# First mixer of a hybrid backbone step: decay tables by blocks on ScalarE, softmax scaling on ScalarE, SiLU held until the decay exponentials, attention's copies behind retention

## The chip, the cores and the metric

The program runs on one core of a Trainium2 chip. The metric is the device time of one launch in microseconds (us). The engines have short names in the profile: PE is TensorE (matmul; PEld is its weight load), DVE is VectorE, ACT is ScalarE, POOL is GpSimd, SP is SyncE, which here issues nearly all of the DMAs. Below, `hp` is a pair of heads (0 to 3), so hp1 is the second pair.

## The reference, cut to what matters

One inference step over two layers, for 256 latent and 128 context tokens of width 1024, all in fp32. Every layer is a mixer and a SwiGLU channel mixer (called FFN below); a conditioned shift, scale and gate and a norm stand before and behind each. The change is in the mixer of layer 0, which runs two groups of eight heads side by side on one input projection:

```python
z = h @ w_in                       # qa, ka, va | qb, kb, vb, gb
# attention: local window with a position bias, plus the context, in one softmax
s = jnp.concatenate([s_loc, s_ctx], axis=-1)
p = jax.nn.softmax(s, axis=-1)
o = p_loc @ v_loc + p_ctx @ v_ctx
# retention, forward and backward, per head with decay log_g < 0
diff = pos[:, None] - pos[None, :]
dmask = where(diff >= 0, exp(log_g * diff), 0)
o = (q @ k.T * dmask) @ v + (q * q_dec) @ state
ob = _rmsnorm(o_f + flip(o_b)) * silu(gb)
out = concatenate([oa, ob]) @ w_out
```

## The kernel before

All 384 tokens stay in SBUF, features on the partitions. A product with a weight matrix keeps fp32 accuracy by splitting: the weight chunk `wr` (8 tiles of 128x128) becomes `wh`, a rounded copy that ACT makes (line 244), plus `wl`, the rest, which DVE makes by a subtraction (line 252); the activation is `hh` plus `hl` in the same way. Each tile then costs three matmuls, hh by wh, hh by wl and hl by wh (line 226). 216 weight chunks of 512 KB pass through three buffers.

A second kind of weight, `mraw` (1 MB chunks in two buffers), gives the conditioning. Most of its chunks are worked off by DVE with a multiply and sum (`mscr<-mraw,msb`, line 265), as filler work of low priority; the pair of chunks 16 and 17 and the pair 18 and 19 go to PE instead (`bank<-mraw,sc`, four or eight rows at a time, function `mod_pe`), and the small product `ca,mev` finishes a pair.

The mixer of layer 0 runs these products in turn: queries and keys of attention (E1), its values (E2), values of retention (E5), the last of attention's queries (E3), queries and keys of retention (E4), the gate (E6), and then the output product (OUT). Beside them run small generators, one instruction at a time: `attention(hp)`, `probabilities(h)` (bias, maximum, exponentials, then the scaling of the 128x896 table `as` by the reciprocal sums `sm`, three line 258 instructions), `attended(hp)`, `retention(hp)`, `retention_norm`, `gate_out` (SiLU of the gate `va`, 128x1536) and `attention_out` (the copies hh and hl of attention's output `qa`).

`retention(hp)` first gets the keys and queries with their halves swapped by eight small DMAs (`ro<-qk`), rotates on DVE (`ro<-ro,cse`, `qk<-qk,cse`, `qk<-qk,ro`), multiplies the queries by their decay (`qd<-qd,qk`; PE uses it in `qd,s`), and then builds for each of its two heads a 128x384 table of decays, `dt` in the code and `scr` in the profile: a line 258 instruction multiplies the forward distances E_DP by the head's rate, a line 265 instruction adds the backward distances E_DM times the other rate, ACT takes the exponential of the whole, and an identity is added in the middle 128 columns. In the left 128 columns all forward distances are 0, in the right 128 all backward ones. The table masks the products of queries and keys (`qk 64x256` on PE, then `ro<-bank,scr` and `at<-bank,scr` on DVE), and `ro,vb` and `at,vb` multiply by the values.

`retention_norm` follows when all four pairs are there: a sum of squares on PE (`scr,cse 32x96`), a square root on ACT, a reciprocal and a spreading on DVE, and for each pair a broadcast on PE (`scr,cse 128x384`), two multiplications on DVE (the second by the SiLU of the gate) and the copies hh and hl. OUT's second half needs these. Behind OUT stands the Step: the norm after the mixer, the addition to `x`, and the norm before the FFN, with `acc,ca`, `rs,cb` and others as its small products. Some `cb,ca` products there have no use for the result; they only keep PE busy.

What comes first on each engine is set in the Python program, before the kernel runs: each generator is a stream with a priority, and a planner (`Machine.run`, a list scheduler) again and again emits the instruction that could start first by its own table of costs, at ties the one with the smaller priority number. On the chip each engine runs its list in that order, and waits on semaphores for what its instruction needs. So a change of the cost, kind or priority of a few instructions in one stream can reorder the lists from there on, and the planner's clock carries it into later stages. Attention has priority 3.0, retention 3.5, `retention_norm`, `gate_out` and `attention_out` 2.5, weight splitting 1 or 6, and the filler on DVE 8. A DMA is on SP's one list.

Of the kernel before, what the change touches and what calls it, by code (L numbers as in the profile page):

```python
# [32 lines left out]
AF = mybir.ActivationFunctionType  # L33
# [3 lines left out]
P = 128  # L37
# [4 lines left out]
NT = NS + NP  # L42
# [435 lines left out]
def emit_all(nc, tc, ctx, io, outs):  # L478
    cp = ctx.enter_context(tc.tile_pool(name="cp", bufs=1))
    pp = ctx.enter_context(tc.tile_pool(name="pp", bufs=1, space=bass.MemoryType.PSUM))  # L480
    M, I = Machine(), Build(nc)
    MUL, ADD, SUB = ALU.mult, ALU.add, ALU.subtract
# [622 lines left out]
            ev.add(("gb", m - 24))  # L1105
        banks.give(b)

    L0.attended = L0.exps = 0

    def attention(hp):  # L1110

# [11 lines left out]
    def probabilities(h, res, b0, b1):  # L1123
        s, mx, sm = res
        yield lambda: len(L0.biases) > 0 and L0.biases[0][0] == h
        bias = L0.biases.popleft()[1]
        yield I.tt(s[:, 0:NT], b0[:, :NT], bias[:, 0], ADD)
        yield I.reduce_max(mx[:, 2:3], b0[:, NT:512])
        yield I.tt(s[:, NT:768], b1[:, :NT], bias[:, 1], ADD)
        banks.give(b1)  # L1130
        L0.bias.give(bias)
        yield I.reduce_max(mx[:, 0:2], s[:, :768].rearrange("p (t c) -> p t c", t=2))
        yield I.ts(mx, mx, -1.0, MUL)
        yield I.act(s[:, 768:896], b0[:, NT:512], AF.Exp, bias=mx[:, 2:3], accum=sm[:, 2:3])
        banks.give(b0)
        for tb in range(2):
            t = s[:, NT * tb:NT * tb + NT]
            yield I.act(t, t, AF.Exp, bias=mx[:, tb:tb + 1], accum=sm[:, tb:tb + 1])
        L0.exps += 1
        yield I.recip(sm, sm)  # L1140
        for c0, c1, n in ((0, NT, 0), (NT, 768, 1), (768, 896, 2)):
            yield I.ts(s[:, c0:c1], s[:, c0:c1], sm[:, n:n + 1], MUL)
        pt, = yield from L0.pt.take()
        b0, b1 = yield from banks.take(2)
        for kb in range(2):
            for tb in range(2):
                c = NT * tb + P * kb
                yield I.transpose(b0[:, 256 * kb + P * tb:256 * kb + P * tb + P], s[:, c:c + P], ident)
        yield I.act(pt[:, :512], b0)
        banks.give(b0)  # L1150
        for n, c in enumerate((256, NT + 256, 768)):
            yield I.transpose(b1[:, P * n:P * n + P], s[:, c:c + P], ident)
        yield I.act(pt[:, 512:], b1[:, :NT])
        banks.give(b1)
        L0.heads.give(res)
        L0.ptof[h] = pt
        if 2 * (h // 2) in L0.ptof and 2 * (h // 2) + 1 in L0.ptof:
            M.spawn(attended(h // 2), 3, margin=M_ATT)

    L0.ptof = {}  # L1160

    def attended(hp):

# [16 lines left out]
    def retention(hp):  # L1180

        res, = yield from L0.ret.take()
        s0, kd, ro, qd, at = res
        st = at[:, 0, :P]
        yield lambda: "ret" in ev
        yield I.dma(s0, io["s0r"][:, hp])
        ap_, ats = kd.rearrange("p a b c -> p (a b c)").rearrange("p (a b) -> p a b", a=2), (ro, at)
        yield lambda: "ret" in ev and ("qb", hp) in ev and ("kb", hp) in ev and len(L0.vb_in) == 3
        qk, vb, cse = L0.qk, L0.vb, L0.cse
        q, k = qk[:, hp, 0], qk[:, hp, 1]  # L1190

        for a in range(0, P, 16):
            yield I.dma(ro[a:a + 16], qk[a ^ 16:(a ^ 16) + 16, hp, :, :NS])

        b, = yield from banks.take()
        yield I.transpose(b[:, :P], k[:, NS:NT], ident)
        yield I.tt(kd, b[:, :P].rearrange("p (j c) -> p j c", j=2).unsqueeze(2).to_broadcast([P, 2, 2, 64]),
                   L0.kdec[:, 2 * hp:2 * hp + 2].unsqueeze(3).to_broadcast([P, 2, 2, 64]), MUL)
        yield tuple(I.mm(b[:, P + 64 * j:P + 64 * j + 64], kd[:, j].rearrange("p a b -> p (a b)"),
                         vb[:, 2, 64 * (2 * hp + j):64 * (2 * hp + j) + 64]) for j in range(2))  # L1200
        yield I.act(st, b[:, P:NS])
        banks.give(b)
        yield I.dma(outs["sret"][:, P * hp:P * hp + P], st)

        lat = qk[:, hp, :, :NS]
        wide = lambda o: cse[:, o:o + NS].unsqueeze(1).to_broadcast([P, 2, NS])
        yield I.tt(ro, ro, wide(E_SIN), MUL)
        yield I.tt(lat, lat, wide(E_COS), MUL)
        yield I.tt(lat, lat, ro, ADD)

        for d, e0 in ((0, E_TF), (1, E_TB)):
            yield I.act(qd[:, d], cse[:, e0:e0 + NS], AF.Exp, scale=L0.rdp[:, hp, d:d + 1])
        yield I.tt(qd, qd, q[:, :NS].unsqueeze(1).to_broadcast([P, 2, NS]), MUL)
        po, = yield from banks.take()
        for d in range(2):
            yield I.mm(po[:, :NS], s0[:, d], qd[:, d], d == 0, False)

        rows = [slice(64 * j, 64 * j + 64) for j in range(2)]
        dts = yield from scr.take(2)
        for j, dt in enumerate(dts):  # L1220

            h = 2 * hp + j
            yield I.ts(dt, cse[:, E_DP:E_DP + NT], L0.rdb[:, 0, h:h + 1], MUL)
            yield I.stt(dt, cse[:, E_DM:E_DM + NT], L0.rdb[:, 1, h:h + 1], dt, MUL, ADD)
            yield I.act(dt, dt, AF.Exp)
            yield I.tt(dt[:, P:2 * P], dt[:, P:2 * P], ident, ADD)
        bs = yield from banks.take(2)
        yield tuple(I.mm(bs[j][:, NS * n:NS * n + NS], k[rows[j], P * s_:P * s_ + P], q[rows[j], :NS])
                    for n, s_ in ((0, 1), (1, 0)) for j in range(2))
        for j in range(2):  # L1230
            for n in range(2):
                yield I.tt(ats[j][:, n], bs[j][:, NS * n:NS * n + NS], dts[j][:, P * n:P * n + NS], MUL)
        yield tuple(I.mm(bs[j][:, :P], k[rows[j], NS:NT], q[rows[j], NS:NT]) for j in range(2))
        for j in range(2):
            yield I.tt(ap_[:, j], bs[j][:, :P], dts[j][:, P:2 * P], MUL)
        banks.give(*bs)
        scr.give(*dts)
        head = lambda b, j: vb[:, b, 64 * (2 * hp + j):64 * (2 * hp + j) + 64]
        for n, s_ in ((0, 1), (1, 0)):
            yield tuple(I.mm(po[64 * j:64 * j + 64, :NS], head(s_, j), ats[j][:, n], False, n == 1) for j in range(2))  # L1240
        yield tuple(I.mm(po[64 * j:64 * j + 64, NS:NT], head(2, j), ap_[:, j]) for j in range(2))
        L0.exps += 1
        yield I.act(q, po[:, :NT])
        banks.give(po)
        L0.ret.give(res)
        ev.add(("ob", hp))
# [27 lines left out]
        scr.give(t)  # L1274

    def gate_out():
        yield lambda: all(("gb", i) in ev for i in range(4))
        yield I.act(L0.sg, L0.sg, AF.Silu)
        ev.add("silu")

# [340 lines left out]
    with tc.tile_pool(name="l0", bufs=1) as lp:  # L1621
# [13 lines left out]
        for hp in range(4):  # L1635
            M.spawn(retention(hp), P_RET + 0.01 * hp, margin=M_RET)
        M.spawn(retention_norm(), 2.5, margin=M_RN)
        M.spawn(attention_out(), 2.5)
        M.spawn(gate_out(), 2.5)

        def stores():
# [75 lines left out]
```

## Time and profile before

| | us |
|---|---|
| median of 3 runs | 1129.93 |
| lowest and highest run | 1129.28, 1131.42 |
| the profiled execution's own time | 1129.32 |
| its span in the trace | 1127.5 |

The profile is of one execution. Times in its rows count from the start of its span. "Busy" is the time in which at least one instruction of an engine ran; "idle before" is the time an engine stood still ahead of an instruction, and "<-" says which engine or transfer ended that wait. PEclk is TensorE's granted clock as a share of its full 2.4 GHz. The last row of a wait list counts "us in total, times, longest us". The first mixer's attention and retention lie at about 57 to 198 us, its norm and the output product at 198 to 241, the Step at 241 to 252, the first FFN follows to 590, the second layer's mixer lies at 590 to 800, and the last FFN ends the span.

### The profile page before, as it was taken

How to read it: one execution, taken by the hardware profiler on the slowest of the kernel's cores; microseconds unless marked ns; L12 is line 12 of the kernel's file. 1: busy time of each engine (PE TensorE's matmuls, PEld its weight loads, DVE VectorE, ACT ScalarE, POOL GpSimd, SP SyncE). 2: the span in 40 equal slices, each digit the busy share in tenths (PEclk: the TensorE clock that was granted, in tenths of full speed). 3: DMA queues.
4: the chain of work that ended last, by engine and by line, in shares of the span. 5: the costliest groups of instructions: out<-in, count | busy, mean ns of one | idle time of the engine just before them, and what ended most of it. 6: DMA issues, size and time to landing. Idle time of an engine off the chain costs nothing.

```text
span 1127.5 us, 18541 instructions
## 1 busy us (share of the span) xinstructions
PE 1088.1 (97%) x7180; PEld 1011.7 (90%) x7180; DVE 819.9 (73%) x1524; ACT 541.8 (48%) x1002; POOL 136.7 (12%) x143
## 2 busy tenths in 40 slices
PE   6999999899999999999999999999999999999996
PEld 5778888679999999999887988888989999999995
DVE  2598888687989999995888489996786444444334
ACT  3585555368333333323765456655666333333321
POOL 1220000000000000234024046352000000000001
PEclk9999999999999999999999999999999999999998
DMA  9966544534667677565341322223224333333431
GB/s 351 359 215 215 168 149 132 215 136 152 233 241 240 238 245 240 205 227 167 135 156 62 127 85 85 76 76 103 94 84 141 122 123 129 123 123 129 131 112 56
DMA packets 49688, 180.44 MB, mean 160 GB/s; under 512 B 6560, under 2 KB 13728, under 8 KB 43072
## 3 DMA queue, kind: packets, MB, share of 16 engines
q1 hardware_dynamic: 49536, 179.18, 46.7%
q8 instruction: 56, 0.92, 0.3%
q14 instruction: 32, 0.26, 0.1%
q0 software_dynamic: 64, 0.08, 0.0%
HBM read 174.79 MB, written 3.41 MB: 158 GB/s over the span
## 4 chain that ended last, share of the span: by engine, by line
PE 77%; DVE 15%; issue 3%; DMA 2%; ACT 1%; SPq 1%; POOL 0%; DVEq 0%; ACTq 0%; POOLq 0%
PE bank L226 76%; DVE wl L252 3%; DVE mscr L265 2%; DMA mraw<-in_w_mod 2%; DVE XB L252 1%; DVE XA L252 1%; SPq L291 1%; DVE TA L252 1%; DVE scr L258 1%; PE bank L230 1%; DVE scr L252 1%; DMA ro<-qk 0%; DVE ZW L252 0%; DVE ac L282 0%; POOL ZW L250 0%
## 5 line engine op out<-in xcount | busy, mean ns | idle before, releaser
L226 PE MATMUL bank<-hh,wh 128*128 128x384 f32 (+1 forms) x1248 | 431.0, 345 | 0.0
L226 PE MATMUL bank<-hh,wl 128*128 128x384 f32 (+1 forms) x1248 | 425.4, 341 | 0.0
L226 PE MATMUL bank<-hl,wh 128*128 128x384 f32 (+1 forms) x1248 | 391.0, 344 | 0.0
L252 DVE TENSOR_TENSOR wl<-wr,wh 128x1024 fp32r<-128x1024 f32 x216 | 272.5, 1262 | 128.2 <-ACT wh L244 128.0
L244 ACT ACTIVATE wh<-wr 128x1024 fp32r<-128x1024 f32 x216 | 228.1, 1057 | 151.2 <-PE bank L226 106.0
L226 PEld LDWEIGHTS bank<-hh,wh 128*128 128x128 f32 x1248 | 237.9, 191 | 6.4 <-ACT scr L244 2.4
L226 PEld LDWEIGHTS bank<-hh,wl 128*128 128x128 f32 x1248 | 237.5, 190 | 0.9 <-issue 0.3
L226 PEld LDWEIGHTS bank<-hl,wh 128*128 128x128 f32 x1248 | 232.4, 189 | 5.6 <-issue 2.0
L265 DVE SCALAR_TENSOR_TENSOR mscr<-mraw,msb 128x1024 bf16<-128x1024 f32 x128 | 159.4, 1245 | 3.5 <-ACT msb L244 2.4
L226 PE MATMUL bank<-gh,wl 128*128 128x384 f32 x352 | 118.2, 336 | 1.8 <-DVE wl L252 1.8
L226 PE MATMUL bank<-gh,wh 128*128 128x384 f32 x352 | 117.6, 334 | 0.0
L226 PE MATMUL bank<-gl,wh 128*128 128x384 f32 x352 | 117.6, 334 | 0.0
L226 PEld LDWEIGHTS bank<-gh,wl 128*128 128x128 f32 x352 | 66.1, 188 | 3.4 <-DVE wl L252 3.4
L226 PEld LDWEIGHTS bank<-gl,wh 128*128 128x128 f32 x352 | 66.1, 188 | 0.0
L226 PEld LDWEIGHTS bank<-gh,wh 128*128 128x128 f32 x352 | 66.1, 188 | 0.0
L244 ACT ACTIVATE fs<-bank 128x384 f32<-128x384 f32 x44 | 21.1, 492 | 90.2 <-PE bank L226 90.2
L252 DVE TENSOR_TENSOR fs<-bank,fs 128x384 f32<-128x384 f32 x44 | 24.1, 556 | 39.4 <-PE bank L226 39.4
L244 ACT ACTIVATE gh<-fs 128x384 fp32r<-128x384 f32 x44 | 22.5, 519 | 57.7 <-DVE fs L252 57.6
L244 ACT ACTIVATE scr<-bank 128x384 f32<-128x384 f32 x44 | 21.9, 499 | 58.2 <-PE bank L226 58.2
L250 POOL TENSOR_TENSOR rB<-x,fy 128x384 f32<-128x384 f32 x1 | 1.9, 1877 | 387.3 <-DVE fy L258 387.3
L250 POOL TENSOR_TENSOR x<-x,fy 128x384 f32<-128x384 f32 x4 | 4.5, 1152 | 346.4 <-DVE fy L252 346.4
L250 POOL TENSOR_TENSOR ZW<-XB,TA 128x192 f32<-128x192 f32 x48 | 37.9, 810 | 31.8 <-ACT XA L244 17.4
(249 smaller groups left out, 1330.1 us busy)
## 6 DMA issues: line engine op xcount, KB each, us to landing
mraw<-in_w_mod SPq DMA_DIRECT2D x48, 1024.0 KB, 5.7
wr<-in_w_ffn_in SPq DMA_DIRECT2D x88, 512.0 KB, 3.3
wr<-in_w_ffn_out SPq DMA_DIRECT2D x44, 512.0 KB, 3.3
wr<-in_w_in_odd SPq DMA_DIRECT2D x40, 512.0 KB, 3.3
wr<-in_w_in_even SPq DMA_DIRECT2D x28, 512.0 KB, 4.4
wr<-in_w_out_even SPq DMA_DIRECT2D x8, 512.0 KB, 4.0
wr<-in_w_out_odd SPq DMA_DIRECT2D x8, 512.0 KB, 3.3
bias<-in_bias SPq DMA_DIRECT2D x8, 384.0 KB, 3.8
```

The costliest lines, as they stand in the source:

```text
L226: return Op("PE", lambda: self.nc.tensor.matmul(out, lhsT=lhsT, rhs=rhs, start=start, stop=stop), [out], [lhsT, rhs], cost + 0.004)
L230: return Op("PE", lambda: self.nc.tensor.transpose(out, in_, ident), [out], [in_], 0.11)
L244: return Op("ACT", lambda: self.nc.scalar.activation(out, in_, func, **kw), outs, ins, 0.1 + width(in_) / 1200, table)
L250: return Op("POOL", lambda: self.nc.gpsimd.tensor_tensor(out=out, in0=a, in1=b, op=op), [out], [a, b], 0.12 + n * 0.0021)
L252: return Op("DVE", lambda: self.nc.vector.tensor_tensor(out=out, in0=a, in1=b, op=op), [out], [a, b], 0.06 + n / 960)
L258: return Op("DVE", lambda: self.nc.vector.tensor_scalar(out=out, in0=a, scalar1=s1, scalar2=s2, op0=op0, **kw), [out], ins, 0.19 + width(o ...
L265: return Op("DVE", lambda: self.nc.vector.scalar_tensor_tensor(out=out, in0=a, scalar=s, in1=b, op0=op0, op1=op1, **kw), outs, ins, 0.1 + ...
L291: return Op("SP", lambda: self.nc.sync.dma_start(out, in_), [a for a in here if a is out], [a for a in here if a is in_], n / 355e3)
```

## The change

Four edits, all in the mixer of layer 0. In `probabilities`, the scaling of the two 128x384 parts of a softmax table goes from DVE to ACT (a copy with a scale that is read per partition); the third, 128x128, stays. In `retention`, the decay table is built by blocks: DVE's two instructions and the addition of the identity work on the middle 128 columns alone, the left and the right block are each one exponential on ACT that takes the rate as its scale, and the middle gets an exponential of its own. In `gate_out`, the SiLU waits, in the planner, until all eight decay tables and all four pairs' query decays have been planned. `attention_out` has priority 3.6 where it had 2.5.

```diff
@@ attention's probabilities
         yield I.recip(sm, sm)
-        for c0, c1, n in ((0, NT, 0), (NT, 768, 1), (768, 896, 2)):
-            yield I.ts(s[:, c0:c1], s[:, c0:c1], sm[:, n:n + 1], MUL)
+        for tb in range(2):
+            yield I.act(s[:, NT * tb:NT * tb + NT], s[:, NT * tb:NT * tb + NT], scale=sm[:, tb:tb + 1])
+        yield I.ts(s[:, 768:896], s[:, 768:896], sm[:, 2:3], MUL)
@@ retention
             yield I.act(qd[:, d], cse[:, e0:e0 + NS], AF.Exp, scale=L0.rdp[:, hp, d:d + 1])
+        L0.qds += 1
...
-            yield I.ts(dt, cse[:, E_DP:E_DP + NT], L0.rdb[:, 0, h:h + 1], MUL)
-            yield I.stt(dt, cse[:, E_DM:E_DM + NT], L0.rdb[:, 1, h:h + 1], dt, MUL, ADD)
-            yield I.act(dt, dt, AF.Exp)
-            yield I.tt(dt[:, P:2 * P], dt[:, P:2 * P], ident, ADD)
+            mid = dt[:, P:2 * P]
+            yield I.ts(mid, cse[:, E_DP + P:E_DP + 2 * P], L0.rdb[:, 0, h:h + 1], MUL)
+            yield I.stt(mid, cse[:, E_DM + P:E_DM + 2 * P], L0.rdb[:, 1, h:h + 1], mid, MUL, ADD)
+            yield I.act(dt[:, :P], cse[:, E_DM:E_DM + P], AF.Exp, scale=L0.rdb[:, 1, h:h + 1])
+            yield I.act(dt[:, 2 * P:NT], cse[:, E_DP + 2 * P:E_DP + NT], AF.Exp, scale=L0.rdb[:, 0, h:h + 1])
+            yield I.act(mid, mid, AF.Exp)
+            yield I.tt(mid, mid, ident, ADD)
+            L0.decays += 1
@@ gate_out
-        yield lambda: all(("gb", i) in ev for i in range(4))
+        yield lambda: all(("gb", i) in ev for i in range(4)) and L0.decays == 8 and L0.qds == 4
         yield I.act(L0.sg, L0.sg, AF.Silu)
@@ the streams of the mixer
-        M.spawn(attention_out(), 2.5)
+        M.spawn(attention_out(), 3.6)
```

The lists of the engines move with it. A row of a list is the line of the code, the operation, what it writes and reads, and the columns. The first place is the norm of retention on PE. Before, this stands there (the last pair's mask products, then conditioning chunks and the norm; `hh` and `wh` are products of OUT):

```order
L226 MATMUL bank_66<-ro_157,vb 64x256
L226 MATMUL bank_66<-at_159,vb 64x256
L226 MATMUL bank_66<-kd_156,vb 64x128 x2
L226 MATMUL bank_70<-mraw_104,sc 32x256 x8
L226 MATMUL bank_65<-scr_95,cse 32x96 x4
L226 MATMUL bank_63<-scr_94,cse 128x384
L226 MATMUL bank_70<-mraw_105,sc 32x256 x8
L226 MATMUL bank_66<-scr_94,cse 128x384
L226 MATMUL bank_68<-hh,wh_110 128x384
```

After the change the sum of squares stands among the products of the gate, and this is the start and the end of the 27 products between it and the first broadcast:

```order
L226 MATMUL bank_70<-hh,wh_110 128x384
L226 MATMUL bank_70<-hh,wl_113 128x384
L226 MATMUL bank_65<-scr_94,cse 32x96 x4
L226 MATMUL bank_70<-hl,wh_110 128x384
...
L226 MATMUL bank_69<-hl,wh_111 128x384
L226 MATMUL bank_68<-hl,wh_111 128x384
L226 MATMUL bank_66<-scr_91,cse 128x384
```

Of the 27, the first 16 end the gate (bank_70) and 11 begin OUT; 24, 12 and 17 more stand between the four broadcasts. The conditioning chunks have left this place.

The second place is the retention of hp1 on PE, from its last products of queries and keys (`qk 128x128`) to the products with the values (`ro_157,vb`). Before:

```order
L226 MATMUL bank_67<-qd_153,s_150 128x256
L226 MATMUL bank_70<-qk 128x128
L226 MATMUL bank_69<-qk 128x128
L226 MATMUL bank_67<-qd_153,s_150 128x256
L226 MATMUL bank_66<-hh,wh_110 128x384
L226 MATMUL bank_66<-hh,wl_113 128x384
L226 MATMUL bank_66<-hl,wh_110 128x384
L226 MATMUL bank_66<-hh,wh_110 128x384
L226 MATMUL bank_66<-hh,wl_113 128x384
L226 MATMUL bank_64<-ro_157,vb 64x256
```

After:

```order
L226 MATMUL bank_69<-qk 128x256
L226 MATMUL bank_68<-qk 128x256
L226 MATMUL bank_64<-hl,wh_112 128x384
L226 MATMUL bank_67<-mraw_104,sc 32x256 x4
L226 MATMUL bank_69<-qk 128x128
L226 MATMUL bank_68<-qk 128x128
L226 MATMUL bank_67<-mraw_104,sc 32x256 x4
L226 MATMUL bank_70<-ro_157,vb 64x256
L226 MATMUL bank_70<-at_159,vb 64x256
```

The first of the conditioning chunks now stands here in two halves, and five products have left. Its load is issued by SP right behind the eight DMAs for the swapped halves of the next pair, hp2. It was so before too, but there PE needed the chunk some 40 us later. Chunk 17 has its first four rows in the retention of hp2 and its last four at the start of the Step.

The third place is DVE between the rotation of hp0 (`qk,ro_152`) and the multiplication `qd_153`. Before:

```order
L252 TENSOR_TENSOR qk<-qk,ro_152 128x2x256
L252 TENSOR_TENSOR mod_80<-mod_80,gn 128x4
L265 SCALAR_TENSOR_TENSOR mscr_132,macc_133<-mraw_104,msb_131 128x1024
L252 TENSOR_TENSOR wl_115<-wr_109,wh_112 128x1024
L252 TENSOR_TENSOR as_140<-bank_67,bias_146 128x384
...
L252 TENSOR_TENSOR as_143<-bank_68,bias_147 128x384
L252 TENSOR_TENSOR qd_153<-qd_153,qk 128x512
```

After:

```order
L252 TENSOR_TENSOR qk<-qk,ro_152 128x2x256
L265 SCALAR_TENSOR_TENSOR mod_80<-mod_80,gn 128x2
L265 SCALAR_TENSOR_TENSOR mscr_132,macc_134<-mraw_105,msb_131 128x1024
L252 TENSOR_TENSOR qd_153<-qd_153,qk 128x512
L265 SCALAR_TENSOR_TENSOR mscr_132,macc_134<-mraw_105,msb_131 128x1024
L252 TENSOR_TENSOR as_140<-bank_70,bias_146 128x384
```

So `qd` stands ahead of the next attention pair's work on DVE, and not behind most of it.

In the Step, no `cb,ca` product stands behind the second `rs,cb` any more; the `ca,mev` of chunks 16 and 17 stands ahead of the first `rs,cb` there, and that of chunks 18 and 19 is behind the FFN's first 16 products, where it stood in the Step before.

## Rows read from the trace of the kernel before

**Rows 1.** The page's busy times and its chain of work that ended last.

```profile
PE 1088.1 (97%) x7180; PEld 1011.7 (90%) x7180; DVE 819.9 (73%) x1524; ACT 541.8 (48%) x1002; POOL 136.7 (12%) x143
...
PE 77%; DVE 15%; issue 3%; DMA 2%; ACT 1%; SPq 1%; POOL 0%; DVEq 0%; ACTq 0%; POOLq 0%
```

**Rows 2.** Busy time by stretch; the columns are the stretch and its length, then the busy time of PE, PEld, DVE, ACT and POOL (with instructions), the granted clock, the DMA share and GB/s.

```profile
85.00:135.00 50.00, 50.00 (x313) 42.64 (x311) 42.22 (x88) 26.82 (x60) 0.00 (x0) 1.00 0.61 198
135.00:198.00 63.00, 60.76 (x385) 52.42 (x384) 56.45 (x120) 34.03 (x66) 0.00 (x0) 1.00 0.45 143
198.00:212.00 14.00, 10.59 (x83) 6.32 (x81) 11.39 (x22) 5.75 (x8) 0.00 (x0) 0.94 0.77 288
241.00:252.00 11.00, 8.30 (x145) 5.34 (x134) 7.98 (x19) 4.66 (x11) 0.00 (x0) 0.97 0.55 192
590.00:800.00 210.00, 206.82 (x1774) 183.04 (x1773) 172.34 (x407) 122.47 (x290) 78.50 (x93) 1.00 0.27 89
```

**Rows 3.** A conditioning chunk and the norm of retention, in order of time: start, duration, engine, line, operation, what it writes and reads, and in brackets the idle time before it.

```profile
204.21 1.07 PE L226 MATMUL bank<-mraw,sc 128*32 128x256 f32 x16
...
205.38 1.28 ACT L244 ACT_TABLE_LOAD   x1
205.41 0.37 PE L226 MATMUL bank<-scr,cse 128*32 128x96 f32 x8
...
206.68 0.34 ACT L244 ACTIVATE rs<-bank,eps 128x96 f32<-128x96 f32 x1
...
207.84 0.56 DVE L252 TENSOR_TENSOR scr<-rs,cb 128x384 f32<-128x384 f32 x1
...
208.45 0.91 PE L226 MATMUL bank<-scr,cse 128*128 128x384 f32 x2 [2.66 <-DVE scr L252]
```

**Rows 4.** The same columns as rows 2, for three short stretches at that place.

```profile
205.40:208.40 3.00, 0.37 (x8) 0.16 (x8) 2.39 (x3) 1.60 (x2) 0.00 (x0) 1.00 0.79 265
...
210.40:213.80 3.40, 3.40 (x15) 2.14 (x8) 1.72 (x4) 1.12 (x2) 0.00 (x0) 0.50 1.02 419
213.80:217.00 3.20, 3.20 (x21) 2.93 (x21) 0.95 (x5) 0.53 (x1) 0.00 (x0) 1.00 0.47 195
```

**Rows 5.** The Step, in order of time, PE and DVE.

```profile
247.94 1.05 PE L226 MATMUL bank<-ca,mev 128*128 128x2 f32 x8
...
248.92 0.43 PE L226 MATMUL bank<-cb,ca 128*32 128x128 f32 x8
249.41 0.56 DVE L252 TENSOR_TENSOR scr<-x,bank 128x384 f32<-128x384 f32 x1 [1.49 <-PE bank L226]
...
250.74 0.55 DVE L252 TENSOR_TENSOR scr<-x,bank 128x384 f32<-128x384 f32 x1 [0.77 <-PE bank L226]
...
251.35 0.65 PE L226 MATMUL bank<-cb,ca 128*32 128x128 f32 x8 [0.68 <-DVE scr L252]
...
251.93 0.69 PE L226 MATMUL bank<-hh,wh 128*128 128x384 f32 x1
```

**Rows 6.** DVE's instructions between 79 and 205 us, by line, operation and shape: count, busy us, mean ns, idle before.

```profile
L258 DVE TENSOR_SCALAR as<-as,sm 128x384 f32<-128x384 f32 x16 | 6.0, 416 | 0.0
L265 DVE SCALAR_TENSOR_TENSOR scr<-cse,rdb,scr 128x384 f32<-128x384 f32 x8 | 4.9, 610 | 0.0
L258 DVE TENSOR_SCALAR scr<-cse,rdb 128x384 f32<-128x384 f32 x8 | 3.3, 415 | 0.0
...
L252 DVE TENSOR_TENSOR ro<-ro,cse 128x512 f32<-128x512 f32 x4 | 2.8, 692 | 8.4 <-DMA ro<-qk 8.4
...
L252 DVE TENSOR_TENSOR scr<-scr,cb 128x128 f32<-128x128 f32 x8 | 2.3, 288 | 0.3 <-ACT scr L244 0.3
L258 DVE TENSOR_SCALAR as<-as,sm 128x128 f32<-128x128 f32 x8 | 2.2, 281 | 0.0
```

**Rows 7.** The same columns for ACT between 79 and 214 us.

```profile
L244 ACT ACTIVATE as<-as,mx 128x384 f32<-128x384 f32 x16 | 9.7, 611 | 0.0
...
L244 ACT ACTIVATE scr<-scr 128x384 f32<-128x384 f32 x8 | 4.2, 522 | 3.3 <-DVE scr L265 3.3
...
L244 ACT ACTIVATE as<-bank,mx 128x128 f32<-128x128 f32 x8 | 2.9, 364 | 8.4 <-DVE mx L258 8.4
...
L244 ACT ACTIVATE at<-bank 128x128 f32<-128x128 f32 x4 | 1.1, 277 | 1.1 <-PE bank L226 1.1
```

**Rows 8.** PE around the retention of hp1: the last product with the values of hp0, two neighbouring products further on, whose starts give the pitch, and the first products of queries and keys of hp1.

```profile
155.53 0.38 PE L226 MATMUL bank<-ro,vb 128*64 128x256 f32 x1
...
164.57 0.33 PE L226 MATMUL bank<-hh,wh 128*128 128x384 f32 x1
164.74 0.34 PE L226 MATMUL bank<-hh,wl 128*128 128x384 f32 x1
165.01 1.13 PE L226 MATMUL bank<-qk 64*128 64x256 f32 x8
```

**Rows 9.** What PE waited for between 57 and 198 us: total, times, longest.

```profile
PE bank L226 <- DVE qd L252: 1.7, 1, 1.7
```

**Rows 10.** SP's DMA issues in order of time around the swapped halves of hp2.

```profile
155.99 5.06 SPq L291 DMA_DIRECT2D ro<-qk  x8
161.15 0.53 SPq L291 DMA_DIRECT2D mraw<-in_w_mod  x1
```

**Rows 11.** How long the conditioning chunks issued between 145 and 250 us took from issue to landing.

```profile
DMA to landing us min/median/max: 4.8/5.0/7.6
```

More of the change, by code (lines that the diff above doesn't have):

```diff
@@ L1106, in ev_even @@
         banks.give(b)
-    L0.attended = L0.exps = 0
+    L0.attended = L0.exps = L0.decays = 0
     def attention(hp):
@@ L1160, in emit_all @@
     L0.ptof = {}
+    L0.qds = 0
     def attended(hp):
```

## Prediction

> **What bounds the kernel now.** I read the page's totals first, then busy time by stretch, then PE's waits inside the first mixer, and last the two places where PE stands still, instruction by instruction. PE is busy 97% of the span and most of the chain that ended last is PE's [rows 1]. So nothing that is taken from DVE or ACT counts in itself; it counts only where PE waits for it. By stretch, PE idles 0.0 us of 50 in the first part of attention and 63 − 60.76 = 2.2 us from 135 to 198; 14 − 10.59 = 3.4 us at the norm of retention; 11 − 8.30 = 2.7 us in the Step; 3.2 us in the second layer's mixer [rows 2]. The reader is to see that the change, which touches one mixer, can take back at most some 8 us of idle PE plus what the clock loses there, and can add new waits wherever the lists have moved.
>
> The norm of retention is the largest gap. The sum of squares starts on PE at 205.41, ACT meanwhile loads the square root's table, and square root, reciprocal and spreading follow one by one, so that PE stands 2.66 us before the first broadcast at 208.45 [rows 3]. In the 3 us from 205.4 PE is busy 0.37 us. From 210.4 the granted clock is 0.50, the lower of its two levels (1.2 GHz), for 3.4 us, and then 1.00 again [rows 4]. In the Step, DVE's two additions wait 1.49 and 0.77 us for PE, whose list there holds `ca,mev` (1.05 us) and the `cb,ca` products ahead of what DVE needs; the FFN's first product starts at 251.93 [rows 5].
>
> **The change part by part.**
>
> *Scaling and tables.* DVE loses 16 × 0.416 = 6.7 us of scaling. Each table loses 0.415 + 0.610 and gets two instructions on 128 columns, priced by the nearest rows at 0.281 and 0.288: 0.455 less, 3.6 us for eight [rows 6]. In all DVE loses 10.3 us. ACT gains 16 copies with a scale per partition. No row shows that form; the bounds are the exponential on 384 columns without one (0.522) and with one (0.611), and I take 0.6. Each table gets three exponentials on 128 columns, between 0.277 (a copy of that width) and 0.364 (an exponential that reads a bias), in place of one of 0.522: 0.31 to 0.57 more [rows 7]. ACT gains 10.8 to 14.3 us, and I take the upper end. It lies beside PE's work: ACT is busy 26.8 of 50 and 34.0 of 63 us there [rows 2], so 52 us are free. I count nothing for either by itself; if that cover fails, the price is the 14.3 us, rival 3 below.
>
> The Trainium skill (ScalarE: Activation LUTs, Rules for kernel authors) says that multiplications belong on VectorE and not on ScalarE. The rows agree as to the price, 0.416 on DVE against about 0.6 on ACT; by that rule alone the edit would lose 16 × 0.2 = 3 us of engine time, and it would be a loss of time only where ACT and not DVE is late for PE.
>
> *A, the norm.* In the new order 27 products stand between the sum of squares and the first broadcast. At a pitch of 164.74 − 164.57 = 0.17 us [rows 8] they take 4.7 us, and the chain from 205.41 to 208.45 takes 3.0 us [rows 3]. So the wait is covered with 1.7 us to spare, and the later broadcasts, with 12 to 24 products (2.1 to 4.2 us) between them, are covered as well. What could be late next is the SiLU: it now runs behind the square root and the gate's last products, with a second table load (1.28 [rows 3]), and the second multiplication needs it. But OUT's first 48 products use attention's half alone; PE comes to the first product that needs a normed pair some 11 us behind the sum of squares, and ACT's list up to the end of the SiLU sums to about 7.5. The gap of 3.4 us goes. The half clock goes with it: in 3.4 us at half speed PE does what takes 1.7 at full speed; the first products there waited in part for ACT and DVE, so I take 1.5. **A = −3.4 − 1.5 = −4.9.** Bounds: 0 if the same chain only moves to another place, −5.1.
>
> *B, the conditioning chunks.* Sixteen rows of `mraw` on PE leave the norm; they cost the same elsewhere, except for the last four rows of chunk 17 and the `ca,mev` of the pair, which move into the Step, where PE is idle anyway. They are worth 0.5 (half of a chunk's 1.07) and 1.05 [rows 3, 5]. **B = −1.5**, bounds 0 and −1.6.
>
> *C, the wait for qd.* PE waits 1.7 us for the first `qd` [rows 9], which stands on DVE behind a filler, a weight split and five instructions of an attention pair; now it stands behind one filler. **C = −1.7**; bounds 0 and −1.7.
>
> *D, new waits.* PE now needs chunk 16 in the retention of hp1. SP issues its load behind the eight DMAs for hp2's swapped halves. These can't start before hp0's buffer is free: before, they began at 155.99, right after PE's last product with the values of hp0, took 5.06 us to issue, and the load's issue began at 161.15 [rows 8, 10]; it lands 5.0 us later [rows 11]. That is 10.2 us after the start. In the new list PE has, from the same point to the first row of chunk 16: 29 products (5.1 us at the pitch above), four products of queries and keys (1.1 [rows 8]), and small ones for hp0 and hp2, some 1.0, with about 0.7 for the changes between kinds, 7.9 in all. PE waits 2.3 us, and everything behind it on PE's list waits too, the products for the values of hp1 first. Three further places are ties by the rows: DVE's rotation waits 8.4 us in all for the same small DMAs [rows 6], and in the new list PE comes to the products of hp0, hp2 and hp3 within about 1 us of the end of DVE's work for them. I put 1.7 on these together, the size of the one such wait that there is [rows 9]. **D = +4.0**; bounds 0, if the load is issued earlier than before, and 8.4, if all of DVE's wait becomes PE's.
>
> *E, the Step.* Without `cb,ca` behind the second `rs,cb`, DVE need not wait 1.49 and 0.77 us for PE. The second wait lies partly beside ACT's work for the first product, so I take 1.9 of the 2.3. The `ca,mev` of chunks 18 and 19 now falls into the FFN's products and costs its 1.05 there. **E = −0.9**; bounds +1.05 and −1.2.
>
> *Downstream.* The FFN's list is unchanged. The list of the second layer's mixer differs in places, because the planner's clock reaches it shifted. PE idles 3.2 us there [rows 2], so I take 0, with bounds of 1.5 either way.
>
> **The sum** is −4.9 − 1.5 − 1.7 + 4.0 − 0.9 = −5.0 us. The profiled execution took 1129.32 itself (span 1127.5), which gives 1124.3; the median of the runs is 0.6 above it, so I predict 1124.6 for the median.
>
> **The rivals.**
>
> 1. *No new waits.* The load for chunk 16 comes in time, and DVE, 10.3 us lighter, is early at all four pairs. For it: DVE is busy 56.45 of 63 us from 135 to 198 [rows 2], the fullest stretch it has, so relief there is real. Against it: the issue order of the load on SP hasn't changed, only PE's need of it comes earlier. D shrinks to about 0.3, and the time is 1124.6 − 3.7 = 1120.9.
>
> 2. *The transfers take it all back.* All of the 8.4 us that DVE waits for the small DMAs [rows 6] falls on PE, because its list has fewer other products left to run between the pairs, and a thin stretch there brings another spell at half clock such as the one at 210.4 [rows 4], 1.7 us. Then +8.4 + 1.7 against −4.9 − 1.5 − 1.7 − 0.9 = −9.0: +1.1, 1130.7 on the median's scale, no change that can be measured.
>
> 3. *ScalarE becomes the bound; slower.* ACT makes `wh`, PE's next weights, in its one list, and the added copies and exponentials stand ahead of it. If ACT is late at each of them, its 14.3 us fall on PE one for one: −9.0 + 14.3 = +5.3, 1135.2. It decides once ACT's list has no idle time left ahead of a weight copy: with half of the 14.3 on the path the sum is −1.9, and from 11.3 on the kernel is slower by what can be told. Against it: ACT is 54% busy in these 113 us [rows 2], and the list of PE's waits there, whose longest row is DVE's [rows 9], names nothing of ACT. It is the way in which the rule of the Trainium skill named above (ScalarE: Activation LUTs, Rules for kernel authors) would come true.
>
> 4. *The second layer's mixer.* Its new order doubles PE's idle time there: +3.2 [rows 2], 1127.8.
>
> That the change doesn't do what it says I leave out: the new lists show each of its edits.
>
> **How the numbers follow.** A measurement of this kernel can tell about 0.2%, 2.3 us, from no change. Chances: the forecast 0.46, with its own range of 1122 to 1127.3; rival 1 0.18; rival 2 0.16; rival 4 0.09; rival 3 0.11. Faster by over 0.2% (below 1127.7) are nearly all of the forecast (0.45), rival 1, and half of rival 4: 0.68. Within 0.2%: most of rival 2 (0.13), the rest of rival 4 and 0.01 of the forecast: 0.19. Slower: rival 3 and the upper end of rival 2: 0.13. The range from 1120 to 1131 leaves out rival 3, the upper end of rival 2 and the lower end of rival 1, about 0.2.
>
> **What would show it.** A: between the sum of squares and the first broadcast PE has no idle time, and no half clock follows. B: the last four rows of chunk 17 and a `ca,mev` lie in the Step's idle time. C: no wait for `qd` in hp0. D: PE waits about 2.3 us for a DMA of `mraw` in hp1, and up to 2 us in all for `ro`, `at` or `qd` of DVE in the others. E: the stretch from the Step's first `acc,ca` to the FFN's first product is some 2 us shorter. If PE's waits from 57 to 198 us name `wh` or `pt` of ACT, rival 3 is at work; if they sum to more than 9 us, rival 2. The prediction is wrong if the gap at the norm stays, or if a new wait larger than 4 us shows that none of these names.

## The result and the profile after

The change took 1124.46 us in the median (1122.49 to 1125.88, 6 runs), against 1129.61 for the kernel before beside it; the ratio is 0.995, 95% interval 0.9935 to 0.9964. 1124.6 was predicted. The profiled execution of the change is its fastest, 1122.49 with a span of 1120.3, so differences between the two traces sum to about 2 us more than the medians do. One execution of e10 below took 1838.84 us at a mean granted clock of 0.68; it is in none of the numbers, and as it was the profiled one, e10 has no row in the table.

Busy time by stretch, the columns of [rows 2], first of the kernel before and then of the change. The stretches are cut at the same work: from PE's first product of queries and keys of attention to the first sum of the Step; the Step up to the FFN's first product; the first FFN with the second Step; the second mixer; the third Step with the last FFN.

```profile
71.14:240.76 169.62, 163.97 (x996) 139.93 (x995) 144.65 (x297) 96.31 (x193) 0.00 (x0) 0.99 0.54 177
240.76:251.93 11.17, 8.47 (x146) 5.51 (x145) 7.93 (x20) 4.72 (x11) 0.00 (x0) 0.97 0.54 189
251.93:544.25 292.32, 288.47 (x1733) 284.17 (x1729) 258.33 (x416) 115.69 (x168) 30.69 (x19) 1.00 0.63 216
544.25:826.85 282.60, 279.42 (x2181) 251.23 (x2177) 231.95 (x519) 174.75 (x390) 83.94 (x98) 0.99 0.30 100
826.85:1118.07 291.22, 287.65 (x1753) 284.17 (x1752) 132.65 (x178) 109.50 (x160) 0.00 (x0) 1.00 0.34 112
```

```profile
70.66:235.28 164.62, 161.66 (x980) 138.09 (x979) 136.00 (x279) 105.65 (x224) 0.00 (x0) 0.99 0.51 176
235.28:245.09 9.81, 7.89 (x145) 5.72 (x144) 7.84 (x22) 3.93 (x10) 0.00 (x0) 1.00 0.36 114
245.09:537.75 292.66, 288.53 (x1736) 283.59 (x1736) 257.99 (x416) 117.12 (x172) 30.61 (x19) 1.00 0.64 223
537.75:819.66 281.91, 279.50 (x2184) 251.34 (x2176) 232.75 (x520) 174.68 (x389) 79.15 (x98) 0.99 0.29 100
819.66:1110.78 291.12, 287.67 (x1752) 283.97 (x1751) 132.84 (x178) 109.66 (x161) 0.00 (x0) 1.00 0.32 113
```

The reader is to see that the time came out of two stretches, 5.0 us in the first mixer and 1.4 in the Step, with 0.7 in the second mixer, whose list moved too, and 0.5 ahead of the first mixer (71.14 to 70.66). In the first stretch PE's idle time fell from 5.65 to 2.96 us and its busy time by 2.3; DVE's busy time there fell by 8.7 us and ACT's rose by 9.3, and the end moved by less than either.

The norm of retention after, PE's rows and one stretch of busy time (they answer [rows 3, 4]):

```profile
195.72 0.37 PE L226 MATMUL bank<-scr,cse 128*32 128x96 f32 x8
...
200.82 0.81 PE L226 MATMUL bank<-scr,cse 128*128 128x384 f32 x2
```

```profile
195.70:201.00 5.30, 5.30 (x37) 5.13 (x37) 4.01 (x7) 4.98 (x8) 0.00 (x0) 1.00 0.00 1
```

From the sum of squares to the first broadcast PE is busy all 5.3 us at the full clock. What PE waited for between 57 and 250 us now (before: [rows 9] and the waits in [rows 3, 5]):

```profile
PE bank L226 <- DMA mraw<-in_w_mod: 2.4, 1, 2.4
PE bank L226 <- DVE hl L252: 1.9, 1, 1.9
PE bank L226 <- DVE rs L275: 1.0, 1, 1.0
PE bank L226 <- DVE scr L252: 0.6, 1, 0.6
PE bank L230 <- ACT qk L244: 0.6, 1, 0.6
PE bank L226 <- ACT hh L244: 0.4, 1, 0.4
...
```

The longest is the new one, the load of chunk 16; the wait for `hl` lies at 61 us, ahead of attention and retention. This is the place of the load's wait on PE, and the stretches ahead of the chunk and behind its arrival:

```profile
162.92 0.44 PE L226 MATMUL bank<-hl,wh 128*128 128x384 f32 x1
165.72 1.02 PE L226 MATMUL bank<-mraw,sc 128*32 128x256 f32 x8 [2.36 <-DMA mraw<-in_w_mod]
```

```profile
162.90:165.70 2.80, 0.46 (x3) 0.19 (x1) 2.55 (x5) 2.23 (x4) 0.00 (x0) 1.00 0.98 391
165.70:169.20 3.50, 3.48 (x24) 1.39 (x26) 1.71 (x5) 0.00 (x0) 0.00 (x0) 0.52 0.63 249
```

PE is nearly idle for 2.8 us, and in the next 3.5 us the granted clock is 0.52, nearly all at the lower level. So the norm's gap and its half clock are gone; a smaller gap, and a half clock as long as the one before (3.4 us), stand some 30 us ahead of the norm.

The Step after (it answers [rows 5]):

```profile
242.23 1.13 PE L226 MATMUL bank<-rs,cb 128*128 128x96 f32 x8 [0.98 <-DVE rs L275]
243.29 1.50 PE L226 MATMUL bank<-mraw,sc 128*32 128x256 f32 x24
245.17 0.44 PE L226 MATMUL bank<-hh,wh 128*128 128x384 f32 x1 [0.38 <-ACT hh L244]
```

Conditioning products, which have to run anyway, fill the place of the `cb,ca` ones, and no half clock follows here.

### The profile page after: what moved, and what is told of

Read it like the earlier page. It is cut to its first block, busy times and chain, and to the rows that moved or that the text cites. A ratio compares the mean times of both kernels' runs of the same rounds, so it can differ in the third digit from the quotient of the medians.

```text
span 1120.3 us, 18505 instructions
## 1 busy us (share of the span) xinstructions
PE 1083.7 (97%) x7172; PEld 1008.3 (90%) x7172; DVE 811.7 (72%) x1508; ACT 551.7 (49%) x1034; POOL 131.8 (12%) x143
## 4 chain that ended last, share of the span: by engine, by line
PE 80%; DVE 12%; ACT 3%; issue 2%; DMA 2%; SPq 1%; POOL 0%; DVEq 0%; ACTq 0%; POOLq 0%
PE bank L226 79%; DVE wl L252 2%; DVE mscr L265 1%; DMA mraw<-in_w_mod 1%; ACT scr L244 1%; DVE XB L252 1%; PE bank L230 1%; DVE XA L252 1%; DVE scr L258 1%; DMA msb<-in_cB 1%; SPq L291 1%; DVE scr L252 0%; DVE T L258 0%; DVE XA L258 0%; DVE x L252 0%
```

## The experiments

Beside the run itself, the lists of the programs answer one question. With the first two edits in place, taking back the third, the fourth or both gives the same list on every engine, row for row. So the SiLU's hold and the priority 3.6 change nothing in this kernel; only the scaling and the tables act. Without the tables edit (e2) the priority is not idle: taking it back there moves four of PE's rows and two of DVE's by a few places. The scaling edit all by itself was not run.

The table shows where each kernel's trace differs from that of the kernel before, in us (the start times on PE of the same landmarks subtracted; one execution each). "1st FFN" is the whole of it; "Steps 2, 3" stand ahead of the second mixer and of the last FFN. The traced execution of e12 is the slowest of its six (1124.57).

| | median | 1st mixer | Step 1 | 1st FFN | Steps 2, 3 | 2nd mixer | last FFN |
|---|---|---|---|---|---|---|---|
| the change | 1124.46 | −5.0 | −1.4 | +0.4 | −0.1 | −0.7 | 0.0 |
| e1 tables only | 1137.43 | −2.1 | +0.4 | +8.7 | +0.8 | +0.1 | +1.3 |
| e2 scaling only | 1122.57 | −5.9 | 0.0 | +1.2 | −0.1 | −1.8 | 0.0 |
| e3 copies alone | 1131.93 | −3.2 | −1.0 | +5.7 | +0.8 | −1.5 | +1.3 |
| e4 chunk 16 held | 1131.64 | −5.4 | −0.6 | +7.4 | +0.2 | −0.7 | 0.0 |
| e5 rotation on GpSimd | 1125.10 | −2.9 | −1.4 | 0.0 | −0.1 | −0.3 | 0.0 |
| e6 the change again | 1124.99 | −3.7 | −1.4 | 0.0 | −0.1 | −0.4 | 0.0 |
| e7 e2 without busy products | 1119.34 | −5.9 | −2.5 | +0.3 | −2.9 | −0.5 | +2.5 |
| e8 the scaling twice | 1126.33 | −2.4 | −1.4 | −0.1 | −0.2 | −1.2 | 0.0 |
| e9 before without busy products | 1124.94 | −0.6 | −2.5 | −0.4 | −2.8 | +0.8 | 0.0 |
| e11 e2 with one busy group | 1118.56 | −5.9 | −2.2 | +0.3 | −2.4 | −1.4 | +1.1 |
| e12 e2 with two | 1121.25 | −5.9 | −0.9 | +1.4 | −1.9 | −1.0 | +2.5 |

**e1, the tables edit without the scaling edit.**

```diff
-        for tb in range(2):
-            yield I.act(s[:, NT * tb:NT * tb + NT], s[:, NT * tb:NT * tb + NT], scale=sm[:, tb:tb + 1])
-        yield I.ts(s[:, 768:896], s[:, 768:896], sm[:, 2:3], MUL)
+        for c0, c1, n in ((0, NT, 0), (NT, 768, 1), (768, 896, 2)):
+            yield I.ts(s[:, c0:c1], s[:, c0:c1], sm[:, n:n + 1], MUL)
```

> The change without its first edit: the softmax scaling is back on DVE (6.7 of the 10.3 us return to it), the tables stay on ACT. Theory: only PE's list counts. In this list 30 products stand between the sum of squares and the first broadcast, and the conditioning chunk is not in hp1 but in the Step, which has its old form. So the norm's gap and its half clock go (-4.9), the late load does not arise, and the Step gives nothing: about 1124 us, faster than before by 4 to 6. Rival: the gain is DVE's relief, in proportion, 3.6 of 10.3: 1127.8. Rival: ACT's added work costs, and with less of it the kernel is faster than the change by 1 to 2 us.

Measured: 1137.43, ratio 1.0065 (1.005 to 1.008): slower than before. All three expectations fell. The norm's gap did close, but PE waited 4.3 us for `qd` in the first mixer, and the first FFN took 8.7 us more. In this list, as in e3 and e4, the second pair of conditioning chunks (18 and 19) isn't done by the end of the Step and stands in the FFN's products; e4 shows below what that does.

**e2, the scaling edit without the tables edit** (the diff of `retention` taken back, the rest as in the change).

> The change without its second edit: the decay tables are built on DVE as before, the scaling is on ACT. Theory: in this list 24 products stand between the sum of squares and the first broadcast, chunk 16 is again in the retention of hp1 but three products later, and the Step has its old form. The norm's gap goes (-4.9), the wait for the load stays at 1 to 2.4 us: about 1126. Rival: the gain is DVE's relief in proportion, 6.7 of 10.3: 1126.3, but then without a wait for the load and with part of the norm's gap left in the trace.

Measured: 1122.57, ratio 0.9946 (0.9931 to 0.996): the whole gain, without the tables edit (the priority acts here, too, as said above). Neither expectation was right as to the place: the load is no wait here, and the norm is closed all the same. PE comes to chunk 16 at 169.84 us, 16.0 behind the start of the eight DMAs for the swapped halves, where in the change it was there after 7.9; the load is issued 9.6 us behind that start and lands 4.7 later.

**e3, the kernel before with the last edit alone.**

```diff
-        M.spawn(attention_out(), 2.5)
+        M.spawn(attention_out(), 3.6)
```

> The kernel before with nothing but the last edit, attention's copies at priority 3.6. No work changes its engine. Theory: the list alone closes the gap: 14 products and one conditioning chunk stand between the sum of squares and the first broadcast (3.5 us for a chain of 3.0), so most of A comes, about 1125. Rival: without DVE's relief the last pair of retention is late all the same, the gap only moves in front of the sum of squares, and the time stays at 1129.

Measured: 1131.93, ratio 1.0026 (1.0014 to 1.0039). On the kernel before the priority does act. The gap at the norm closed and opened again a few rows on: PE's one wait from 198 to 215 us is now

```profile
PE bank L226 <- ACT hh L244: 2.4, 1, 2.4
```

for the copy `hh<-qk` of the first normed pair: PE is through OUT's first 48 products, which use attention's half alone. And the second pair of conditioning chunks fell into the FFN.

**e4, the change with chunk 16 held until the last pair of retention.**

```diff
             yield lambda: mods.n < mods.allow and (not W.few or ...
+            yield lambda: mods.n != 8 or ("ob", 3) in ev
             yield lambda: mods.pe and not W.hungry
```

> The change, with the first PE conditioning chunk held in the planner until the last pair of retention is planned. Chunks 16 and 17 then stand in the Step, and the Step has its old form with the cb,ca products behind the second rs,cb. Theory: the wait of 2.4 us for the load in hp1 and the half clock behind it go (together 3.5 to 4), the Step's 1.4 to 2 come back: about 1122.5. Rival: the wait was not the load's but DVE's, which only shows up at the next instruction: no gain in hp1, and 1126 with the Step's loss.

Measured: 1131.64, ratio 1.0023 (1.0014 to 1.0032), 7 us above the change. The load's wait is gone, but in the same retention, at 166.2 us, PE waits 1.6 us for DVE's `ro`, a half clock of 6.8 us follows, and the first mixer is only 0.4 to 1.7 us shorter than in the two traces of the change. The loss lies in the FFN. PE, DVE and ACT there, in order of time:

```profile
268.16 1.93 PE L226 MATMUL bank<-mraw,sc 128*32 128x256 f32 x32
...
270.16 0.60 ACT L244 ACTIVATE mev<-bank 128x512 f32<-128x512 f32 x1 [2.92 <-PE bank L226]
270.81 1.05 PE L226 MATMUL bank<-ca,mev 128*128 128x2 f32 x8 [0.72 <-ACT mev L244]
271.97 0.17 DVE L252 TENSOR_TENSOR mod<-bank,bmod 128x8 f32<-128x8 f32 x1 [3.47 <-PE bank L226]
...
272.84 0.98 ACT L244 ACTIVATE hh<-scr,mod 128x256 fp32r<-128x256 f32 x2 [2.08 <-DVE scr L252]
...
273.88 0.45 PE L226 MATMUL bank<-hh,wh 128*128 128x384 f32 x1 [2.01 <-ACT hh L244]
```

The FFN's next input (`hh<-scr,mod`) needs the shift and scale that chunks 18 and 19 give, so the chain chunk, evacuation, small product, DVE, ACT, PE runs in the open: from 268.16 to 273.88 PE does 3.0 us of conditioning and waits 2.7. The `ca,mev` in it (1.05) lies in the FFN of the change, too, so 4.7 us of the 7.0 between the two FFNs are here. The rest fits a half clock behind the Step, which the change has not: 4.7 us of it lie in this FFN, and an estimate of its cost is half of that, 2.3. So the early place of chunk 16, which costs a wait in hp1, is also what lets the second pair be done within the Step.

**e5, the swapped halves issued by GpSimd.** The planner counts them as SP's, so that all other lists stay.

```diff
+    def dma_pool(self, out, in_):
+        op = self.dma(out, in_)
+        op.call = lambda: self.nc.gpsimd.dma_start(out, in_)
+        return op
...
-            yield I.dma(ro[a:a + 16], ...
+            yield I.dma_pool(ro[a:a + 16], ...
```

> The change with the 32 small DMAs of the swapped halves issued by GpSimd instead of SP; the planner still counts them as SP's, so the lists of PE, DVE and ACT are those of the change, word for word. The load of conditioning chunk 16 no longer stands behind hp2's eight DMAs on SP. Theory: PE's wait of 2.4 us for that load goes, and the half clock that followed it (3.4 us, worth 1.2 to 1.7) with it: 3.6 to 4 us below the change in the first mixer, 1120.5 to 1121. Rival: GpSimd's transfers land later than SP's 2.0 us, DVE's rotation waits longer and PE with it, and nothing is gained or it is slower. Rival: the half clock comes all the same, for another thin stretch, and only 2.4 us are gained.

Measured: 1125.10, ratio 0.9968 (0.9955 to 0.998), against 1124.99 for the change measured beside it (e6): nothing. The wait for `mraw` is gone from the list, and its first row is now

```profile
PE bank L226 <- DVE ro L252: 3.7, 1, 3.7
```

GpSimd's small transfers took

```profile
DMA to landing us min/median/max: 1.8/3.6/6.8
```

against 2.0 in the median from SP. On DVE, hp2's rotation stands ahead of hp1's mask products; it waits for these transfers, and PE, a few rows behind the chunk, waits for the mask products. The half clock came again (at 170.7). The first rival was right: two waits lay side by side, for the load and for the rotation, and whichever is left decides. The 3.7 us are those of the slower transfers; with SP's own, e4 shows the hidden wait at 1.6.

**e6, the change again.**

> The change itself once more, beside the other kernels of this call: 1124.5 in the median, and its executions between 1122 and 1126. With e2, which has the scaling edit without the tables edit and came out at 1122.57, this tells whether the tables edit is worth anything: if the change is again about 2 us above e2, it costs; within 1 us it does nothing.

Measured: 1124.99, ratio 0.9962 (0.9947 to 0.9977). The wait for the load is there again, 2.2 us, and the half clock behind it is 6.8 us long where it was 3.4. With e10 below: the change twice at 0.995 and 0.9962, e2 twice at 0.9946 and 0.9952. Their intervals overlap; the tables edit is worth nothing that can be told here, on top of the others.

**e7, e2 without the busy products behind the second `rs,cb`** (left out in all three Steps; they have no result).

```diff
-            yield tuple(I.mm(o[32 * g:32 * g + 32], ones_d, ident) for g in range(4))
+            ops = tuple(I.mm(o[32 * g:32 * g + 32], ones_d, ident) for g in range(4))
+            if W.norm.r2 is not None:
+                for op in ops:
+                    op.call = lambda: None
+            yield ops
```

> e2 (scaling on ACT, tables on DVE) with the cb,ca products behind the second rs,cb left out in every Step; they are there only to keep PE busy and no result depends on them. Theory of term E: DVE's additions wait for these products on PE, 1.5 and 0.8 us in the first Step, and without them the first FFN product starts 1.5 to 2 us earlier; the second and third Step, where the same waits are 0.4 to 1.0, gain some 1 us each: 1122.6 - 3.5 = 1119. Rival: without them PE is thin there and the clock falls to half behind each Step, 1.2 to 1.7 us each, which takes it back: 1122 to 1123.

Measured: 1119.34, ratio 0.991 (0.9896 to 0.9924). DVE's two additions in the first Step, which waited 1.49 and 0.77 us in [rows 5], are now one row without a wait:

```profile
241.57 1.01 DVE L252 TENSOR_TENSOR scr<-x,bank 128x384 f32<-128x384 f32 x2
```

The Step is 2.5 us shorter and the next two 1.4 each. A half clock stands behind each of the three and gives some of it back, 2.5 us in the last FFN and 1.3 in the second mixer against e2, but not all.

**e8, every scaling copy on ACT followed by a useless second one.**

```diff
+            op.call = lambda part=part, call=op.call: (call(), nc.scalar.activation(part, part, AF.Copy))
```

> The change with every scaling copy on ACT followed by a second, useless copy of the same 128x384 part onto itself, unknown to the planner, so that all lists are the change's but for 16 more ACT instructions of about 0.5 us each, 8 us. Theory: ACT's added work lies beside PE's, 1124.5 and at most 1 us more. Rival (ScalarE as the bound): ACT's time falls on PE one for one, 1132.

Measured: 1126.33, ratio 0.9984 (0.9973 to 0.9996), 1.3 us above the change measured beside it (e6). ACT's rows between 79 and 205 us show the second copies (line 1144) beside the first, and PE's list of waits has a new first row:

```profile
L244 ACT ACTIVATE as<-as,sm 128x384 f32<-128x384 f32 x16 | 9.8, 611 | 1.7 <-DVE sm L275 1.2 <-DVE mod L252 0.5
...
L1144 ACT ACTIVATE as<-as 128x384 f32<-128x384 f32 x16 | 8.4, 525 | 0.5
```

```profile
PE bank L230 <- ACT as L1144: 2.6, 6, 0.7
```

Of 8.4 us more on ACT, 2.6 became waits of PE. ACT isn't the bound, but nearly as much work again as the scaling is not free. In the first mixer this trace is 1.3 to 2.6 us behind the two of the change, and that although no half clock follows the load's wait in it:

```profile
171.48 0.64 PE L226 MATMUL bank<-mraw,sc 128*32 128x256 f32 x8 [2.28 <-DMA mraw<-in_w_mod]
```

```profile
170.00:173.00 3.00, 1.52 (x20) 0.62 (x20) 1.85 (x6) 1.47 (x3) 0.00 (x0) 1.00 1.01 397
173.00:180.00 7.00, 7.00 (x55) 5.96 (x52) 6.68 (x17) 2.07 (x6) 0.00 (x0) 1.00 0.69 237
```

**e9, the kernel before without the busy products** (e7's diff on it).

> The kernel before with the cb,ca products behind the second rs,cb left out in every Step, nothing else. Theory of term E on its own ground: as in e7, some 2.5 us in the first Step and 1.4 in each of the next two, 5.2 in all, less what the half clock behind the second and third Step costs (0.7 and 2.5 in e7): 1128.7 - 2 to 5 = 1124 to 1126.5. Rival: e7 gained by an accident of its lists, and here it is within 1 us of before.

Measured: 1124.94, ratio 0.9964 (0.9952 to 0.9977): as much as the whole change brought. Step 1 is 2.5 us shorter as in e7, so it is these products and not e2's lists. Behind this Step, which ends as in e7 with a wait of PE of 1.0 us for ACT's `hh`, no half clock follows here; e7 has one. The busy products are no sure cure for it either: e2, which has all five groups, has one there.

**e10, e2 again.**

> e2 once more: 1122.6 if the first measurement stands. With the change at 1124.5 and 1125.0, this tells whether leaving the tables on DVE is faster by about 2 us (then the tables edit costs in this kernel), or whether the two are the same within 1 us.

Measured: ratio 0.9952 (0.994 to 0.9964), five executions from 1122.72 to 1125.33; read under e6.

**e11 and e12, e2 with one or two groups of busy products in place of five** (the diff is e11's; e12 has a 2 there).

```diff
-GAPS = (2, 1, 4, 5)
+GAPS = (2, 1, 4, 1)
```

> e2 with one group of four cb,ca products behind the second rs,cb of each Step in place of five. Theory: one group lies ahead of DVE's first addition and is done by then, so the Step is as short as without (8.7 us for the first), and PE is a little less thin: 1119, or up to 2 us less if the half clock behind a Step goes. Rival: the clock falls as in e7, 1119.3.

> The same with two groups. The second group waits for DVE or DVE for it once: theory 0.4 us more per Step than e11 where the clock stays at its higher level in one of the three Steps it is the faster, 1118; else 1120.5.

Measured: 1118.56, ratio 0.9905 (0.9892 to 0.9919), and 1121.25, ratio 0.9934 (0.9919 to 0.9948). With one group the first Step is 8.9 us long, with two 10.3, with none 8.7 and with five 11.2. In these traces, with none, one or two groups, the half clock stands behind all three Steps; with five (e2) only behind the first. e11 and e7 can't be told apart; both beat the kernel before and the change.

## Why the prediction was right

The sum was right, its terms less so, and luck has a part in how close it came: in D two errors cancel, and the traces moved by 0.7 us in the second mixer (0.4 in e6) and 0.5 ahead of the first (0.8), which were no terms. The last step was added up wrongly: 1124.3 and 0.6 make 1124.9 and not 1124.6; the measured median is within 0.5 of both.

*A, −4.9: right in place; its size fits.* The wait is gone and no half clock follows at the norm. PE's idle time in the first stretch fell by 2.7 us, which is what A's gap, C and the load's wait make together (−3.4 − 1.7 + 2.4). That DVE's relief plays a part is not excluded, but e1, e2, e3 and e4 all close this gap too, e3 with no work moved between engines, though there it opens again a few rows on.

*B, −1.5, and E, −0.9.* The first mixer lost the conditioning work as said. For the Step E had −1.9, and −1.4 came, with conditioning work in the place of the busy products. That these products held DVE up is shown by e7 and e9: 2.5 us in this Step where nothing takes their place. The half clock behind the Step in the kernel before, which the change's Step has not, was no term.

*C, −1.7: right.* PE's list of waits has no `qd` any more.

*D, +4.0: the right number by a wrong addition.* The load's wait was 2.36 us, where 2.3 was worked out. But the ties with DVE, put at 1.7, hardly came; what came was 3.4 us at half clock behind that wait (6.8 in e6, none in e8), which the sum did not have. PE's remaining query-key products, the chunk's second half and the next `ro,vb` ran in it; an estimate of its cost is 1.7 us at most, half of its length. And D was counted as a cost alone. e4 shows that the same early chunk saves some 5 us in the FFN, and 7 with the half clock that e4 has behind its Step; with the chunk held back to the Step the change is 0.2% slower than the kernel before. No step of the prediction asked by when a chunk's result is needed.

*Scaling and tables.* ACT's prices were right: 0.611 for the copy with a scale, 2 × 0.393 + 0.301 − 0.522 = 0.57 more for a table by these rows of ACT in the change:

```profile
L244 ACT ACTIVATE scr<-cse,rdb 128x128 f32<-128x128 f32 x16 | 5.6, 393 | 0.0
...
L244 ACT ACTIVATE scr<-scr 128x128 f32<-128x128 f32 x8 | 2.4, 301 | 0.0
```

The Trainium skill (ScalarE: Activation LUTs, Rules for kernel authors) would keep the scaling on VectorE. The traces agree as to the price, 0.2 us apiece dearer on ACT, and the kernel with the scaling on ACT and the tables on DVE (e2) is faster than before all the same, since the price on ACT was not what PE waited for.

*Rival 3* is excluded at the change's own load: of 8.4 us more on ACT (e8), PE waited for 2.6, and the list of the change names ACT with 1.0 us in all.

*Downstream:* the second mixer gained 0.7 of its −1.5 to +1.5.

What stays open: executions of the same change lie 3.4 us apart, and traces of it differ by 1.3 us in the first mixer with the same lists (e6), where the half clock is 3.4 us longer. After the same wait for the load, 2.2 to 2.4 us, the half clock lasted 3.4 us in the change, 6.8 in e6 and did not come in e8. So it isn't the rows of a list alone that decide, and what does is not shown. The mean granted clock was 0.993 in the two fastest of six and 0.990 to 0.992 in the others; where the spells fell in the executions without a trace is not known.

## What to carry to other kernels

A change of engine or priority in a kernel with a planned order is a change of the order: read the new lists first, and undo edits in the planner before any run, since two of these four did nothing. When a piece of work moves earlier into a wait, ask also who needs its result and when; its old place may have been the last one in time. Two waits that end together hide each other, so that removing one shows little (e4, e5). And products that only keep an engine busy can hold up the engine that reads the same bank, where the program keeps the two in order: leaving them out was worth as much as the whole change.

## What was not expected of the hardware

DVE's addition reads columns 0 to 383 of a PSUM bank, and the busy products write columns 384 to 511 of it; the addition waited for them all the same (1.49 us in [rows 5], none in e7). This is the program's order and not shown to be the bank's doing: in the trace the addition at 249.41 waits for the semaphore that the last of these products ahead of it raises, and in e7 for one that the last `rs,cb` raises. The planner's own table goes by columns and doesn't have this wait. Small transfers landed in 3.6 us in the median from GpSimd's queue against 2.0 from SP's, though GpSimd issued them as fast (507 ns against 592). The half clock of the change's first mixer came behind a wait of PE of 2.4 us, in the trace of e6 behind one of 2.2; in e8 none came behind one of 2.3.
